# A hybrid diffusion layer on one core: HGRN2's backward direction held in reversed order, scores by 64-row products, split tiles moved to 64 bytes modulo 128

## The chip, the cores and the metric

The kernel runs on one core of one Trainium2 chip. The metric is the device time of one execution in microseconds (us), lower is better.

## The reference, cut to what matters

One layer serves 256 context tokens and 2048 latent tokens of width 1024. `h = RMSNorm(x) * (1 + scale) + shift`, `z = h @ w_in` feeds four groups of heads (convolution, gMLP, HGRN2, S5), their outputs go through `w_out`, and a squared-ReLU MLP of width 4096 follows. Almost all arithmetic is in the matrix products. The part that the change rewrites is HGRN2, a linear recurrence with a forget gate, run forwards and backwards over the same `q` and `v`:

```python
def step(S, inp):
    qc, kc, vc, lf = inp
    b = jnp.cumsum(lf, axis=1)
    b_end = b[:, -1]
    inter = jnp.einsum('blhk,bhkv->blhv', qc * jnp.exp(b), S)
    decay = jnp.where(lower, jnp.exp(diff), 0.0)
    scores = jnp.einsum('bthk,bshk,btshk->bhts', qc, kc, decay)
    intra = jnp.einsum('bhts,bshv->bthv', scores, vc)
    ...
o_f, s_f = hgrn_scan(q, k_f, v, lf_f, s0[:, 0])
o_b, s_b = hgrn_scan(jnp.flip(q, 1), jnp.flip(k_b, 1), jnp.flip(v, 1), jnp.flip(lf_b, 1), s0[:, 1])
```

## The kernel before, in words

**Split products.** Every large product is in three parts: each operand is split into `hi` (rounded to fp32r) and `lo` (the rest), and `gemm_cm` (L185) adds hi*hi, lo*hi and hi*lo for eight slices of 128, so one output of 128 x n takes 24 matmuls at lines L192 to L194. The weights' unit (`whl`, four buffers) is the stationary operand, the tokens' `hi` and `lo` tiles are the moving one, n = 512 columns for a latent block and 256 for the context block. In `gemm_tm` (L576, L579 to L581) and in pass 2's L1096 to L1098 it is the other way round: `whl` moves, and a 128-column slice of the tokens' tile is stationary.

**Blocks and stages.** There are five blocks: the context (256 tokens) and four latent ones (512 each). Pass 1 makes q, v and the gates of HGRN2 and the S5 input and runs `hgrn_local` (L735) for each block and each of two pairs of heads, ten times in all; this lies at about 190 to 630 us. Pass 2 and the S5 scan follow to about 1050 us. From then on it is `mix_out`, `mlp_up` and `mlp_down`: block 0 first (256 columns wide), then blocks 1 to 4. Per latent block `mix_out` has 8 outputs, and each of four quarters has 8 of `mlp_up` and 8 of `mlp_down`; the last quarter of the last block is done in two halves of 256 columns.

**HGRN2 inside a chunk.** `hgrn_local` holds both directions at once, forward in partitions 0 to 63 and backward in 64 to 127, on tiles of 128 x 1024 (two heads by 512 tokens; 512 wide for the context). Scores in a chunk of 128 are built in seven levels (cs = 1, 2, ... 64). In each level a copy `z` of q is made in which the half that must not count is zero (`qz` and `qzr`; ScalarE at L780 and L781, zeros by GpSimd at L778 and L779); eight matmuls of 128 rows, 128 x 128 out, follow (L787); kt is multiplied by the decays in two halves (VectorE for the forward rows, GpSimd for the backward rows, both L791), q likewise (VectorE, L792 and L793), and the scores of the level are taken out of PSUM under a mask (L808, all 1024 columns) or, in the last two levels, by copies (L806). Two instances are interleaved by hand with the products of the next pairs (L1375 on), and the tile framework orders each engine's queue from a simulated timeline.

```python
            A.activation(v4(z, 0, 64, 1), v4(q, 0, 64, 1), AF.Copy)
            A.activation(v4(z, 64, 128, 0), v4(q, 64, 128, 0), AF.Copy)
            ...
                    PE.matmul(sc[:, s_], kt[:, s_], z[:, s_], start=True, stop=True)
```

**Queues.** SyncE issues nearly all DMAs. `hgrn_local` loads q from qn by four DMAs of 64 partitions (L749) and stores q by one (L810).

**Where tiles lie.** Pools are stacked from the low end of a partition (left) or from its high end (right), each tile rounded up to 32 bytes. By that count `whl` starts at 64 modulo 128. The `hi` and `lo` tiles of `hp` (pass 1, pass 2, and block 0's `mix_out`), `h30` (block 0's MLP) and `h3b` (`mlp_down`'s input, blocks 1 to 4), all on the right, start at 96 modulo 128. Those of `h3a`, on the left, which hold the input of `mix_out` and `mlp_up` for blocks 1 to 4, start at 0 modulo 128.

Of the kernel before, what the change touches and what calls it, by code (L numbers as in the profile page):

```python
# [36 lines left out]
CH = 128  # L37
# [37 lines left out]
def trunk_kernel(ctx, tc, I, O):  # L75
# [28 lines left out]
    def psc():  # L104
        return psums["s"].tile([128, 1024], F32, tag="ps", name=nm("psc"))
# [498 lines left out]
    def f_out(b, h, ps, f):  # L604
        n = BLOCKS[b][1]
        v = f[:, (h % 2) * n:(h % 2 + 1) * n]
        A.activation(v, ps[:, :n], AF.Sigmoid)
        A.activation(v, v, AF.Identity, bias=lb[:, h:h + 1], scale=omlb[:, h:h + 1])
# [13 lines left out]
    def pass1_g(b, pair, hs, p1):  # L622


        n = BLOCKS[b][1]
        ps = pg()
        gemm_cm(ps, n, kept_unit("w_p1c", 3 * pair), hs)
        qn = q_out(b, ps, p1)
        f = f_tile(p1)
        for hh in range(2):  # L630
            ps = pg()
            gemm_cm(ps, n, kept_unit("w_p1c", 3 * pair + 1 + hh), hs)
            f_out(b, 2 * pair + hh, ps, f)
        return qn, f
# [100 lines left out]
    def hgrn_local(b, pair, qn, f, vt, p1, qz, Sx, masks_):  # L735
# [6 lines left out]
        def w(tag):  # L742
            return p1.tile([128, 1024], F32, tag=tag, name=nm(tag), bufs=2)

        kt, q, at = w("kt"), w("q"), w("at")
        f = f[:, :n2]
        for hh in range(2):
            for d in range(2):
                SP.dma_start(q[64 * d:64 * d + 64, hh * n:(hh + 1) * n], qn[hh * 64:hh * 64 + 64, :n])  # L749
        G.tensor_scalar(kt[:, :n2], f, -1.0, 1.0, ALU.mult, ALU.add)  # L750
        V.tensor_scalar(f, f, F_MIN, None, ALU.max)
        sc = psc()
        for i in range(m2):
            s_ = slice(i * 128, i * 128 + 128)
            PE.matmul(sc[:, s_], kt[:, s_], q[:, s_], start=True, stop=True)
# [6 lines left out]
        for lv in range(7):  # L762
# [3 lines left out]
            def v4(t, lo_, hi_, half):  # L766
                return t[lo_:hi_, :n2].rearrange("p (m two c) -> p m two c", two=2, c=cs)[:, :, half, :]
# [3 lines left out]
            def tb(lo_, hi_, half):  # L771
                return tv[lo_:hi_, :, half:half + 1].to_broadcast([64, mm, cs])

            if lv < len(qz):
                z = qz[lv]
            else:
                z = p1.tile([128, 1024], F32, tag="qzr", name=nm("qzr"), bufs=2)
                G.memset(v4(z, 0, 64, 0), 0.0)  # L778
                G.memset(v4(z, 64, 128, 1), 0.0)  # L779
            A.activation(v4(z, 0, 64, 1), v4(q, 0, 64, 1), AF.Copy)  # L780
            A.activation(v4(z, 64, 128, 0), v4(q, 64, 128, 0), AF.Copy)  # L781
            sc = psc()
# [32 lines left out]
        A.activation(kt[:, :n2], pt[:, :n2], AF.Copy)  # L815
# [242 lines left out]
    def pass2(b, p2, hp, hs, Sx, gates, gmg, gmw, gmb):  # L1058
# [29 lines left out]
        sr = p2.tile([128, 8], F32, tag="sr", name=nm("sr"))  # L1088
# [226 lines left out]
    psum(ctx, g=3, a=1)  # L1315
    e2 = ExitStack()
# [3 lines left out]
    with ExitStack() as e1:  # L1320
# [292 lines left out]
```

## Time and profile before

| what | value |
|---|---|
| median of 3 runs | 2869.5 us (2867.88 to 2870.06) |
| profiled execution's own time | 2869.65 us |
| span of the trace (first to last instruction) | 2867.9 us, so 1.75 us lie around it |
| mean granted TensorE clock | 0.98 |
| busy shares | TensorE 95%, weight load 78%, VectorE 66%, ScalarE 39%, GpSimd 32% |

PE is TensorE's matmul, PEld its weight load, DVE VectorE, ACT ScalarE, POOL GpSimd, SP SyncE. Matmuls overlap and their ends are modelled, so the time of a matmul in a stream is read from start to start, not from its duration. An fp32 matmul shows as two records, an fp32r one as one.

### The profile page before, as it was taken

To read this page: it belongs to the slowest core of one execution; us is meant where nothing else is said; L and a number is where in the kernel's file an instruction comes from. 1 tells how busy PE (TensorE), PEld (TensorE's weight loads), DVE (VectorE), ACT (ScalarE), POOL (GpSimd) and SP (SyncE) were. 2 spreads that over 40 slices of the span, in tenths; PEclk is the share of its full clock that TensorE was granted. 3 is DMA by queue.
4 is the path that set the end of the run, shared out by engine and by line. 5 is a ranking of instruction groups with operands and counts; after the bars stand their busy time and mean duration, and the time that the engine had idled before them with its cause. 6 is when DMAs were issued, how large, how long until landed. Compare 5 with 4: busy or idle time off the path is not lost.

```text
span 2867.9 us, 38038 instructions
## 1 busy us (share of the span) xinstructions
PE 2711.8 (95%) x14376; PEld 2247.5 (78%) x14376; DVE 1887.3 (66%) x2766; ACT 1109.4 (39%) x1710; POOL 915.7 (32%) x807
## 2 busy tenths in 40 slices
PE   6798999899999869999999999999999999999998
PEld 3576878887777759987788888788887888888888
DVE  8879677966799986669873474943474334553336
ACT  4645454541432535442422343333343223433223
POOL 4435234622443533343221242211432111411113
PEclk8899999999999989999999999999999999999999
DMA  7884555678887746633333443333343334333334
GB/s 263 281 293 151 173 192 175 224 275 320 288 291 246 240 165 212 185 114 113 113 103 96 125 143 107 111 96 107 113 148 101 99 95 126 95 125 96 96 96 126
DMA packets 186279, 467.17 MB, mean 163 GB/s; under 512 B 40176, under 2 KB 70000, under 8 KB 173040
## 3 DMA queue, kind: packets, MB, share of 16 engines
q1 hardware_dynamic: 183936, 463.56, 49.3%
q8 instruction: 114, 1.87, 0.3%
q10 hardware_dynamic: 2160, 1.18, 0.1%
q14 instruction: 69, 0.57, 0.1%
HBM read 383.47 MB, written 77.53 MB: 161 GB/s over the span
## 4 chain that ended last, share of the span: by engine, by line
PE 59%; DVE 12%; DMA 3%; issue 1%; ACT 0%; POOL 0%; SPq 0%; DVEq 0%; ACTq 0%
PE pg L194 19%; PE pg L193 19%; PE pg L192 19%; DVE x L1184 3%; DVE m L997 1%; DVE whl L162 1%; DVE gg L1005 1%; DVE hh L1014 1%; DVE pa L289 1%; DMA x<-uD 1%; DMA whl<-w_p2c_hl 1%; DVE hh L1013 0%; DMA x<-in_xT_dram 0%; DVE lo L304 0%; PE pb L1051 0%
## 5 line engine op out<-in xcount | busy, mean ns | idle before, releaser
L194 PE MATMUL pg<-hi,whl 128*128 128x512 f32 (+1 forms) x3488 | 1287.5, 370 | 8.3 <-DVE whl L162 8.2
L192 PE MATMUL pg<-hi,whl 128*128 128x512 f32 (+1 forms) x3488 | 1284.8, 371 | 10.0 <-ACT whl L156 3.5
L193 PE MATMUL pg<-lo,whl 128*128 128x512 f32 (+1 forms) x3488 | 1287.2, 370 | 4.6 <-DVE lo L1245 3.0
L160 POOL TENSOR_TENSOR whl<-wraw,whl 128x512 fp32r<-128x512 f32 (+1 forms) x296 | 434.2, 1488 | 1199.7 <-ACT whl L156 1133.4
L192 PEld LDWEIGHTS pg<-hi,whl 128*128 128x128 f32 x3488 | 658.2, 189 | 133.0 <-issue 6.6
L193 PEld LDWEIGHTS pg<-lo,whl 128*128 128x128 f32 x3488 | 659.2, 189 | 129.3 <-issue 7.4
L194 PEld LDWEIGHTS pg<-hi,whl 128*128 128x128 f32 x3488 | 659.3, 189 | 127.3 <-DVE whl L162 8.9
L156 ACT ACTIVATE whl<-wraw 128x1024 fp32r<-128x1024 f32 (+1 forms) x396 | 415.5, 1052 | 600.6 <-PE pg L194 459.0
L162 DVE TENSOR_TENSOR whl<-wraw,whl 128x1024 fp32r<-128x1024 f32 x248 | 309.5, 1249 | 65.2 <-ACT whl L156 63.7
L1257 DVE SCALAR_TENSOR_TENSOR x<-pg,adaT,x 128x512 f32<-128x512 f32 (+1 forms) x168 | 111.7, 668 | 290.6 <-PE pg L194 290.3
L1242 DVE TENSOR_TENSOR t<-t 128x512 f32<-128x512 f32 (+1 forms) x160 | 115.7, 724 | 252.4 <-ACT t L1241 252.0
L1241 ACT ACTIVATE t<-pg 128x512 f32<-128x512 f32 (+1 forms) x160 | 88.6, 554 | 367.8 <-PE pg L194 365.4
L1184 DVE SCALAR_TENSOR_TENSOR x<-x,cvw 128x512 f32<-128x512 f32 (+1 forms) x300 | 216.2, 764 | 0.6
L1245 DVE TENSOR_TENSOR lo<-t,hi 128x512 fp32r<-128x512 f32 (+1 forms) x160 | 142.6, 892 | 36.2 <-ACT hi L1244 36.1
L791 POOL TENSOR_TENSOR kt<-kt,tnx 64x256 f32<-64x256 f32 (+1 forms) x120 | 98.7, 830 | 173.8 <-issue 132.7
L252 POOL TENSOR_TENSOR sq<-sq,sq 128x512 f32<-128x512 f32 (+1 forms) x56 | 87.6, 1563 | 124.0 <-ACT sq L248 124.0
L1244 ACT ACTIVATE hi<-t 128x512 fp32r<-128x512 f32 (+1 forms) x160 | 93.0, 582 | 82.8 <-DVE t L1242 82.8
L1225 DVE SCALAR_TENSOR_TENSOR x<-pg,adaT,x 128x512 f32<-128x512 f32 (+1 forms) x40 | 27.8, 694 | 108.6 <-PE pg L194 108.5
L248 ACT ACTIVATE sq<-x 128x512 f32<-128x512 f32 (+1 forms) x120 | 66.0, 553 | 77.3 <-DVE sq L252 17.3
L787 PE MATMUL psc<-qzr,kt 128*128 128x128 f32 x576 | 76.8, 286 | 10.5 <-DVE kt L791 7.2
L787 PEld LDWEIGHTS psc<-qzr,kt 128*128 128x128 f32 x576 | 72.6, 201 | 14.5 <-POOL kt L791 7.9
L303 ACT ACTIVATE hi<-hm,adaT 128x512 fp32r<-128x512 f32 (+1 forms) x72 | 49.5, 697 | 67.3 <-DVE hm L301 63.3
(371 smaller groups left out, 2913.2 us busy)
## 6 DMA issues: line engine op xcount, KB each, us to landing
wraw<-in_mlp_w_dram SPq DMA_DIRECT2D x328, 512.0 KB, 3.6
whl<-w_p2c_hl SPq DMA_DIRECT2D x32, 1024.0 KB, 7.5
whl<-w_p1c_hl SPq DMA_DIRECT2D x22, 1024.0 KB, 7.6
wraw<-in_w_out_dram SPq DMA_DIRECT2D x40, 512.0 KB, 3.6
awt<-in_ada_w_dram SPq DMA_DIRECT2D x32, 512.0 KB, 6.1
whl<-w_p1t_hl SPq DMA_DIRECT2D x12, 1024.0 KB, 5.0
x<-in_xT_dram SPq DMA_DIRECT2D x16, 512.0 KB, 5.8
aw<-in_ada_w_dram SPq DMA_DIRECT2D x8, 1024.0 KB, 6.6
```

The source lines that it names most:

```text
L156: A.activation(hi[:, :w], raw[:, :w], AF.Copy)
L160: G.tensor_tensor(lo[:, h_], raw[:, h_], f32(hi[:, h_]), ALU.subtract)
L162: V.tensor_tensor(lo[:, :w], raw[:, :w], f32(hi[:, :w]), ALU.subtract)
L192: PE.matmul(ps[:, :n], wh, xh[:, ts], start=k == 0, stop=False)
L193: PE.matmul(ps[:, :n], wh, xl[:, ts], start=False, stop=False)
L194: PE.matmul(ps[:, :n], wl, xh[:, ts], start=False, stop=k == 7)
L787: PE.matmul(sc[:, s_], kt[:, s_], z[:, s_], start=True, stop=True)
L791: eng.tensor_tensor(kv, kv, tb(lo_, hi_, 1 - half)[:, hs_, :], ALU.mult)
L1184: V.scalar_tensor_tensor(acc[i][:, :n], u2[:, i, k:k + n], cvw[:, i, k:k + 1], acc[i][:, :n], ALU.mult, ALU.add)
L1242: V.tensor_tensor(r, r, r, ALU.mult)
L1245: V.tensor_tensor(lo, r, f32(hi), ALU.subtract)
L1257: V.scalar_tensor_tensor(x8[:, o, ts], ps[:, :n], adaT[:, 40 + o, c:c + 1], x8[:, o, ts], ALU.mult, ALU.add)
```

## The change

The backward half of every tile of `hgrn_local` is held in reversed order inside each chunk of 128, so that both directions use the same halves at a level. q is loaded twice: qx (both directions in plain order, for the first product) and q (backward half reversed, from qr). kx holds kt's backward half in plain order, remade at each level. Each level's eight products of 128 rows become sixteen of 64 rows, 64 columns each, the forward ones from partitions 0 to 63 and the backward ones from 64 to 127, into different PSUM banks. The zeroed copies of q are gone. The update of kt is one VectorE operation on 128 partitions in place of one on VectorE and one on GpSimd, that of q one in place of two. The transposes at the end are in halves of 64 rows. Apart from that three small tiles move others: `edge` (32 bytes) at the high end moves all right-hand pools by 32 bytes, so `hp`, `h30` and `h3b` start at 64 modulo 128; `pad` (64 bytes) moves `h3a` from 0 to 64; `sr` grows from 32 to 64 bytes, which leaves the tiles of `p2` below it at multiples of 64.

```diff
     def q_out(b, ps, p1):
...
-        return qn
+        qr = p1.tile([128, 512], F32, tag="qr", name=nm("qr"))
+        A.activation(turn(qr, 0, 128, 0, n), chunks(qn, 0, 128, 0, n), AF.Copy)
+        return qn, qr
...
-        A.activation(v, ps[:, :n], AF.Sigmoid)
+        A.activation(v[0:64], ps[0:64, :n], AF.Sigmoid)
+        A.activation(chunks(f, 64, 128, a, a + n), turn(ps, 64, 128, 0, n), AF.Sigmoid)
...
         for hh in range(2):
             for d in range(2):
-                SP.dma_start(q[64 * d:64 * d + 64, hh * n:(hh + 1) * n], qn[hh * 64:hh * 64 + 64, :n])
+                for q_, src in ((qx, qn[0]), (q, qn[d])):
+                    SP.dma_start(q_[64 * d:64 * d + 64, hh * n:(hh + 1) * n], src[hh * 64:hh * 64 + 64, :n])
...
+        A.activation(kx[0:64, :n2], kt[0:64, :n2], AF.Copy)
+        A.activation(chunks(kx, 64, 128, 0, n2), turn(kt, 64, 128, 0, n2), AF.Copy)
...
-                z = p1.tile([128, 1024], F32, tag="qzr", name=nm("qzr"), bufs=2)
-                G.memset(v4(z, 0, 64, 0), 0.0)
-                G.memset(v4(z, 64, 128, 1), 0.0)
-            A.activation(v4(z, 0, 64, 1), v4(q, 0, 64, 1), AF.Copy)
-            A.activation(v4(z, 64, 128, 0), v4(q, 64, 128, 0), AF.Copy)
...
+            def score(d, i):
+                o_ = sc[:, 512 * d + 64 * i:512 * d + 64 * i + 64].rearrange("p (r c) -> p r c", c=cs)
+                s_ = slice(i * 128, i * 128 + 128)
+                if d:
+                    PE.matmul(o_, kt[0:64, s_], v4(q[0:64, s_], 1), start=True, stop=True)
+                else:
+                    PE.matmul(o_, kx[64:128, s_], v4(q[64:128, s_][:, ::-1], 0), start=True, stop=True)
...
                 for i in range(hh * m, hh * m + m):
-                    s_ = slice(i * 128, i * 128 + 128)
-                    PE.matmul(sc[:, s_], kt[:, s_], z[:, s_], start=True, stop=True)
+                    for d in (1, 0):
+                        score(d, i)
...
-                for eng, lo_, hi_, half in ((V, 0, 64, 0), (G, 64, 128, 1)):
-                    kv = v4(kt, lo_, hi_, half)[:, hs_, :]
-                    eng.tensor_tensor(kv, kv, tb(lo_, hi_, 1 - half)[:, hs_, :], ALU.mult)
-            V.tensor_tensor(v4(q, 0, 64, 1), v4(q, 0, 64, 1), tb(0, 64, 0), ALU.mult)
-            V.tensor_tensor(v4(q, 64, 128, 0), v4(q, 64, 128, 0), tb(64, 128, 1), ALU.mult)
+                kv = v4(kt[:, :n2], 0)[:, hs_, :]
+                V.tensor_tensor(kv, kv, tb(1)[:, hs_, :], ALU.mult)
+            A.activation(v5(kx, 1), v5(kt, 0)[:, :, ::-1, ::-1], AF.Copy)
+            V.tensor_tensor(v4(q[:, :n2], 1), v4(q[:, :n2], 1), tb(0), ALU.mult)
...
-                V.copy_predicated(a3, masks_[:, lv, :].unsqueeze(1).to_broadcast([128, m2, 128]), s3)
+                    V.copy_predicated(a5, m5.to_broadcast([128, m2, 64 // cs, cs]),
+                                      s3.rearrange("p m (r c) -> p m r c", c=cs))
...
-        SP.dma_start(qD[b][:, 2 * pair:2 * pair + 2, :], q[:, :n2].rearrange("p (h t) -> p h t", h=2))
+        qo = p1.tile([128, 1024], F32, tag="qo", name=nm("qo"))
+        A.activation(chunks(qo, 64, 128, 0, n2), turn(q, 64, 128, 0, n2), AF.Copy)
+        for lo_, q_ in ((0, q), (64, qo)):
+            SP.dma_start(qD[b][lo_:lo_ + 64, 2 * pair:2 * pair + 2, :],
+                         q_[lo_:lo_ + 64, :n2].rearrange("p (h t) -> p h t", h=2))
...
-            PE.transpose(pt[:, i * 128:i * 128 + 128], kt[:, i * 128:i * 128 + 128], ident)
+            PE.transpose(pt[:, i * 64:i * 64 + 64], kt[0:64, s_], ident[0:64, 0:64])
+            PE.transpose(pt[:, 512 + i * 64:512 + i * 64 + 64], kx[64:128, s_], ident[64:128, 64:128])
...
-        sr = p2.tile([128, 8], F32, tag="sr", name=nm("sr"))
+        sr = p2.tile([128, 16], F32, tag="sr", name=nm("sr"))
...
+    edge = pool(ctx, "edge", side="right").tile([128, 8], F32, tag="edge", name="edge")
+    G.memset(edge, 0.0)
...
+    pad = pool(e5, "pad").tile([128, 16], F32, tag="pad", name="pad")
+    G.memset(pad, 0.0)
     h3a = pool(e5, "h3a", 9)
```

The masked copy at levels 0 to 4 is now done twice (d = 1, 0), each on half of the columns; the copies of levels 5 and 6 keep their number.

## Rows read from the trace of the kernel before

**Rows 1.** The page: busy time by engine, and the granted clock in 40 slices.
```profile
PE 2711.8 (95%) x14376; PEld 2247.5 (78%) x14376; DVE 1887.3 (66%) x2766; ACT 1109.4 (39%) x1710; POOL 915.7 (32%) x807
...
PEclk8899999999999989999999999999999999999999
```
**Rows 2.** Busy time by stage: window, PE, PEld, DVE, ACT, POOL; clock, DMA share, GB/s.
```profile
190.00:640.00 450.00, 405.69 (x2654) 357.75 (x2655) 360.87 (x645) 221.50 (x386) 183.32 (x238) 0.96 0.58 200
640.00:1050.00 410.00, 373.50 (x2475) 300.57 (x2474) 348.96 (x577) 143.71 (x284) 157.95 (x168) 0.97 0.77 260
...
1210.00:2790.00 1580.00, 1574.89 (x6883) 1275.28 (x6882) 863.41 (x963) 531.35 (x703) 406.09 (x267) 1.00 0.35 110
```
**Rows 3.** Line L193 in a stretch of mlp_up, mlp_down, block 0: count, min/median/max, first to last start.
```profile
L193 PE MATMUL pg<-lo,whl x64: 392/392/392, 1960.8 to 2004.1; 128*128 128x512 f32 x64
...
L193 PE MATMUL pg<-lo,whl x64: 389/394/397, 1916.0 to 1960.1; 128*128 128x512 f32 x64
...
L193 PE MATMUL pg<-lo,whl x315: 277/278/281, 1090.0 to 1199.9; 128*128 128x256 f32 x158
```
**Rows 4.** Timeline, TensorE: first and last of 22, then of 41 matmuls with whl moving.
```profile
361.55 0.40 PE L579 MATMUL pg<-whl,hi 128*128 128x512 f32 x1
...
366.45 0.39 PE L581 MATMUL pg<-whl,hi 128*128 128x512 f32 x1
...
814.38 0.28 PE L1096 MATMUL pg<-whl,hi 128*128 128x256 f32 x1
...
819.12 0.28 PE L1097 MATMUL pg<-whl,lo 128*128 128x256 f32 x1
```
**Rows 5.** Groups by line, 190 to 640 us: busy, mean ns, idle before, releasers.
```profile
L791 POOL TENSOR_TENSOR kt<-kt,tnx 64x256 f32<-64x256 f32 (+1 forms) x120 | 98.7, 830 | 173.8 <-issue 132.7 <-PE psc L787 32.9 <-DVE Sl L856 5.9
L787 PE MATMUL psc<-qzr,kt 128*128 128x128 f32 x576 | 76.8, 286 | 10.5 <-DVE kt L791 7.2 <-ACT kt L815 2.1 <-DVE at L808 0.8
...
L808 DVE COPY_PREDICATED at<-masks,psc 128x1024 f32<-128x1024 int32 (+1 forms) x50 | 60.5, 1210 | 0.0
L791 DVE TENSOR_TENSOR kt<-kt,tnx 64x256 f32<-64x256 f32 (+1 forms) x120 | 57.2, 491 | 27.3 <-PE psc L787 26.4
...
L793 DVE TENSOR_TENSOR q<-q,tnx 64x512 f32<-64x512 f32 (+1 forms) x59 | 45.1, 766 | 1.7
...
L780 ACT ACTIVATE qzr<-q 64x512 f32<-64x512 f32 (+1 forms) x40 | 23.5, 587 | 45.4 <-DVE q L792 23.8 <-PE psc L787 18.8 <-POOL kt L791 2.6
```
**Rows 6.** TensorE's waits, 190 to 640 us: us in total, times, longest.
```profile
PE psc L787 <- DVE kt L791: 10.1, 6, 2.9
PE psc L787 <- DVE at L808: 8.5, 8, 3.8
```
**Rows 7.** Timeline, TensorE: into and out of the 64-column products, and 64 columns moving.
```profile
353.95 0.40 PE L192 MATMUL pg<-hi,whl 128*128 128x512 f32 x1
354.28 0.85 PEld L820 LDWEIGHTS psc<-at,vt 128*64 128x64 f32 x16 [0.37 <-issue]
354.28 1.09 PE L820 MATMUL psc<-at,vt 128*64 128x128 f32 x16
355.30 0.52 PEld L787 LDWEIGHTS psc<-qzr,kt 128*128 128x128 f32 x4 [0.17 <-issue]
...
359.30 1.89 PE L829 MATMUL psc<-vt,kt 128*128 128x64 f32 x16
```
**Rows 8.** Groups by line and shape: masked copies; a reversed (L991) and a plain copy.
```profile
L808 DVE COPY_PREDICATED at<-masks,psc 128x1024 f32<-128x1024 int32 x40 | 53.3, 1332 | 0.0
...
L991 ACT ACTIVATE d<-pd 64x512 f32<-64x512 f32 x16 | 9.5, 593 | 0.2
L990 ACT ACTIVATE d<-pd 64x512 f32<-64x512 f32 x16 | 9.4, 589 | 20.7 <-PE pd L986 20.7
...
L808 DVE COPY_PREDICATED at<-masks,psc 128x512 f32<-128x512 int32 x10 | 7.2, 724 | 0.0
```
**Rows 9.** DMA issues, 190 to 640 us: KB each, median us to landing.
```profile
q<-qn SPq DMA_DIRECT2D x24, 128.0 KB, 2.5
```

More of the change, by code (lines that the diff above doesn't have):

```diff
@@ L592, in vt_tile, with chunks, turn @@
         return p1.tile([128, 4, 256], F32, tag="vt", name=nm("vt"), bufs=2)
+    def chunks(t, lo_, hi_, a, e):
+        return t[lo_:hi_, a:e].rearrange("p (m t) -> p m t", t=CH)
+    def turn(t, lo_, hi_, a, e):
+        return chunks(t, lo_, hi_, a, e)[:, :, ::-1]
     def q_out(b, ps, p1):
@@ L605, in f_out @@
         n = BLOCKS[b][1]
[L606 to L607 removed]
+        a = (h % 2) * n
+        v = f[:, a:a + n]
+        A.activation(v[0:64], ps[0:64, :n], AF.Sigmoid)
+        A.activation(chunks(f, 64, 128, a, a + n), turn(ps, 64, 128, 0, n), AF.Sigmoid)
         A.activation(v, v, AF.Identity, bias=lb[:, h:h + 1], scale=omlb[:, h:h + 1])
@@ L733, in trunk_kernel, with hgrn_local @@
     first = []
-    def hgrn_local(b, pair, qn, f, vt, p1, qz, Sx, masks_):
+    def hgrn_local(b, pair, qn, f, vt, p1, Sx, masks_):
         t0, n, c = BLOCKS[b]
@@ L743, in w @@
             return p1.tile([128, 1024], F32, tag=tag, name=nm(tag), bufs=2)
-        kt, q, at = w("kt"), w("q"), w("at")
+        kt, q, at, kx = w("kt"), w("q"), w("at"), w("kx")
+        qx = p1.tile([128, 1024], F32, tag="qx", name=nm("qx"))
         f = f[:, :n2]
@@ L754, in hgrn_local @@
             s_ = slice(i * 128, i * 128 + 128)
-            PE.matmul(sc[:, s_], kt[:, s_], q[:, s_], start=True, stop=True)
+            PE.matmul(sc[:, s_], kx[:, s_], qx[:, s_], start=True, stop=True)
         V.tensor_tensor(q[:, :n2], q[:, :n2], f, ALU.mult)
@@ L764, in hgrn_local, with v4, v5 @@
             mm = n2 // (2 * cs)
-            def v4(t, lo_, hi_, half):
-                return t[lo_:hi_, :n2].rearrange("p (m two c) -> p m two c", two=2, c=cs)[:, :, half, :]
+            def v4(t, half):
+                return t.rearrange("p (m two c) -> p m two c", two=2, c=cs)[:, :, half, :]
+            def v5(t, half):
+                return t[64:128, :n2].rearrange("p (m r two c) -> p m r two c", m=m2, two=2, c=cs)[:, :, :, half, :]
             tv = tcur.rearrange("p (m two) -> p m two", two=2)
-            def tb(lo_, hi_, half):
-                return tv[lo_:hi_, :, half:half + 1].to_broadcast([64, mm, cs])
@@ L774, in hgrn_local, with tb @@
-            if lv < len(qz):
-                z = qz[lv]
-            else:
-                z = p1.tile([128, 1024], F32, tag="qzr", name=nm("qzr"), bufs=2)
-                G.memset(v4(z, 0, 64, 0), 0.0)
-                G.memset(v4(z, 64, 128, 1), 0.0)
-            A.activation(v4(z, 0, 64, 1), v4(q, 0, 64, 1), AF.Copy)
-            A.activation(v4(z, 64, 128, 0), v4(q, 64, 128, 0), AF.Copy)
+            def tb(half):
+                return tv[:, :, half:half + 1].to_broadcast([128, mm, cs])
@@ L1370, in trunk_kernel @@
         masks_ = const("masks", [128, 5, 128], I["masks"], I32, p1, SP)
-        qz = [p1.tile([128, 1024], F32, tag=f"qz{lv}", name=f"qz{lv}") for lv in range(3)]
-        for z in qz:
-            G.memset(z, 0.0)
         prev = None
         for i in range(2 * NB):
-            cur = hgrn_local(P1_ORDER[i // 2], i % 2, *ready[i], p1, qz, Sx, masks_)
+            cur = hgrn_local(P1_ORDER[i // 2], i % 2, *ready[i], p1, Sx, masks_)
             for _ in range(5):
```

20 lines of the change are left out of this document (13 added, 7 removed).

## The prediction, made before the changed kernel had run

> **What bounds the kernel now.** The page's busy shares and clock slices come first: TensorE is busy for 95% of the span and, after the first fifth or so, its clock stands at the full 2.4 GHz level [rows 1]. The table by stage says where that is a bound. From 1210 to 2790 us TensorE is busy 1574.89 of 1580 us while VectorE has 863.41 [rows 2]: that is more than half of the span, and there any time off a matmul comes off the end. In pass 1 (190 to 640 us) TensorE is busy 405.69 of 450 us, so 44 us are idle, and VectorE 360.87; in pass 2 and the scan (640 to 1050 us) VectorE has 348.96 and TensorE 373.50 of 410, and neither alone is the bound [rows 2].
>
> The third view is what a matmul costs in a stream. L193 is every third matmul. In a stretch of mlp_up its 64 starts run from 1960.8 to 2004.1 us: 43.3 us over 63 x 3 steps, 229.1 ns each. In mlp_down they run from 1916.0 to 1960.1: 44.1 over 189, 233.3 ns [rows 3]. Engine, shape, clock, weights' tile and code are the same; the moving tile lies at 0 modulo 128 in the first and at 96 in the second. In block 0, moving tile at 96 and 256 columns, 315 starts take 109.9 us: 116.7 ns, half of 233.3 [rows 3], so the loss goes with the columns that stream. 512 columns at 2.4 GHz would be 213.3 ns.
>
> **The tile offsets.** This is the large part. The change makes the pair (moving, weights) 64/64 in every split product; before it is 0/64 (229.1), 96/64 (233.3) and, where whl moves, 64/96. That last pair takes 4.90 us over 21 steps, 233.3 ns, at 512 columns, and 4.74 over 40, 118.5 ns, at 256 [rows 4]. So 64/64 is in no row. Its bounds are 213.3 ns (columns at full clock) and 233.3 (the slowest pair seen). All three pairs fit one reading: what counts is how far the two tiles are out of step. 32 bytes out costs 233.3 whichever operand is off, 64 bytes out 229.1; in step would be one more step of 4.2, some 224.9. I take 226, most of that step, as it lies nearest to the 0/64 row. For 256 columns I take half, 113.
>
> Counts by the code: mlp_up and mix_out of blocks 1 to 4, 4 x (768 + 192) = 3840 matmuls at 0; mlp_down of the same, 4 x 768 less 192 = 2880 of 512 columns at 96; block 0 (1728) and the split last quarter (384) make 2112 of 256 columns at 96. Gains: 2880 x 7.3 ns = 21.0 us; 3840 x 3.1 = 11.9; 2112 x 3.7 = 7.8. Pass 1 has about 840 products of 512 columns (504 at L192 to L194, 336 at L579 to L581): 840 x 7.3 = 6.1, times the 0.9 of the time that TensorE is busy there, 5.5. Pass 2 has 768; with VectorE as busy as it is, I count a fifth of 5.6, so 1. In the tail nothing else comes up: VectorE's 55% and a DMA share of 0.35 leave room [rows 2]. Sum 47. Each ns by which 64/64 is off my 226 moves the end by 8.7 us (6720 matmuls, half of 2112, nine tenths of 840, a fifth of 768).
>
> **HGRN2, TensorE.** 504 score matmuls of 128 rows become 1008 of 64 rows. Two records each, as before. With 64 columns moving and 128 columns of weights, 16 records took 1.89 us, about 0.11 each [rows 7]; L787's undisturbed step, with 128 moving, is the same 0.11 (its 0.29 is the modelled duration) [rows 5]. If forward and backward halves run side by side, the total stays 504 x 2 x 0.11 = 111 us; if they follow each other it is 222. Halves of columns do run side by side: 16 records of L820, each 128 columns twice over (107 ns at 2.4 GHz), took 1.09 us instead of 1.7 [rows 7]. No row shows halves of rows; I take side by side, and the doubling is a rival. The price of going in and out of half-array products is in the same rows: from the last 128-row matmul to the first of L820 0.33 us instead of 0.23, and 0.17 us of idle weight load after it [rows 7], so 0.27 for a group. The timeline has L787 in 57 groups between other products: 57 x 0.27 = 15 us more. The transposes' 64-row halves I cost at nothing (72 become 144 with half the columns; bounds a few us either way).
>
> **HGRN2, the other engines.** VectorE loses one of the two q updates per level: 70 operations of about 0.76 us, 52 us less [rows 5]. The masked copy becomes two of half width: 2 x 0.724 against 1.332 us [rows 8], 40 times, 5 more; the ten narrower ones add 1. kt's update costs VectorE the same count and loses its GpSimd partner (98.7 us in 120 operations, 0.83 each) [rows 5]. ScalarE loses 140 copies of z (0.59 each [rows 5], some 82 us) and gets 70 reversed copies to kx; a reversed copy costs what a plain one does, 593 against 589 ns [rows 8], so 40 us, and with kx's first copies, qo, qr and the second sigmoid about 83 in all: no change, on an engine with 221.50 of 450 us [rows 2]. SyncE gets 40 more q loads and 10 more q stores; a load takes 2.5 us [rows 9], one more group is queued ahead of the next weights' loads, and at a DMA share of 0.58 [rows 2] it lies under products. If that cover went, it would be 2.5 us for each of ten tiles.
>
> What this is worth is TensorE's idle time in pass 1, 44 us. The waits behind it are named: kt on VectorE 10.1 us, the masked copy 8.5 [rows 6], and L780 waited 23.8 us for the q update [rows 5], which now feeds the product with no copy between. The new link is kt to kx to the backward product, 0.6 us of ScalarE per level, with ScalarE's queue behind it. Bounds: 0 to 40 us back; I take 15, near the named waits' sum. It pays for the 15 of the switches. HGRN2 comes out at 0, from -30 to +20.
>
> **Sum.** 2869.65 (the profiled execution: its span of 2867.9 and 1.75 around it; it stands 0.15 above the median of 2869.5) - 47 + 0 = 2822 us.
>
> **Rivals.**
> *64/64 is as good as 0/64, no better* (only the 32 byte step matters): 229.1 everywhere, 3.1 x 8.7 = 27 later, 2849. For: 64/96 at 256 columns costs 118.5, more than half of its 233.3, as if the weights' 32 bytes added a fixed amount there and the moving 64 were as good as 0 [rows 4].
> *64 is as slow as 96*: 7.3 x 8.7 = 63 later, 2886, slower than before, since h3a's 3840 lose 4.2 each. For: the only rows with a moving tile at 64 stand at 233.3 [rows 4]. Against: their weights lie at 96. It decides from 231.4 ns up.
> *The offset does nothing*; h3a is fast for another reason: 2870. The Trainium skill, SBUF — State Buffer (Specifications), gives 16-byte lines, with a penalty for each access that crosses to a new one; 0, 64 and 96 are all whole lines, and by that the tiles' places would change nothing. Rows 3 speak against it: 229.1 and 233.3 with only the tile differing.
> *64-row halves follow each other*: 111 us more on TensorE in pass 1, of which its idle time takes up some 20: about 90 later, 2912. Against: L820. For: loads of two halves share one path in no row that I have. The Trainium skill, TensorE: Matmul & The Clock Gate (LDWEIGHTS), says that a load's time goes with its columns and not its rows, so a 64-row load would be no shorter; L829's 0.11 for 64 columns moving agrees that the load is what counts there.
>
> **How the numbers follow.** Chances: my case 0.50, as good as 0/64 0.24, nothing 0.08, as slow as 96 0.11, halves in turn 0.07. Over 0.2% (5.7 us, about what a measurement of this kernel tells from no change) faster: 0.49 + 0.23 + 0.02 = 0.74; slower 0.11 + 0.07 + 0.01 = 0.19; within 0.07. My case's own range is 2800 to 2845 (223.5 to 228.6 ns). The whole: down to 2788, where 64/64 is 222, and up to 2886, where it is 233.3; left out are the halves in turn and a still faster pair.
>
> **What would show it.** L193 from start to start in mlp_up and mlp_down: one value for both, 226; 229.1, 233.3 or two different values name the rival. The window of the MLP, 1580 us now, would be shorter by some 34. In pass 1, forward and backward records starting within some 10 ns of each other; L787's successor in groups of 16 records per half level in 0.9 us, not 1.8; GpSimd's share falling by 100 us and more; VectorE's by about 45. The prediction is wrong if the MLP keeps its length, or if pass 1 grows by over 20 us.

## The result, and the profile after

The changed kernel takes 2943.51 us (median of 4 runs, 2938.39 to 2943.9) against 2869.78 for the kernel before beside it: 1.0257 times as long, 95% interval 1.0244 to 1.0269. The forecast was 2822. The profiled execution took 2943.9 us, its span is 2941.8. Two things went otherwise than forecast: TensorE's clock fell in HGRN2, and the new tile offsets were worth nothing.

The page of the changed kernel answers to [rows 1]:

```profile
PE 2786.3 (95%) x15456; PEld 2318.1 (79%) x15456; DVE 1808.9 (61%) x2746; ACT 1109.9 (38%) x1698; POOL 747.8 (25%) x586
...
PEclk8897889879999989999999999999999999999999
```

VectorE lost 78 us and GpSimd 168, more than forecast, but the clock's eights and sevens now reach into the ninth slice and TensorE's busy time rose by 74. The table by stage (columns as in [rows 2], with block 0's start as one row more) says where:

```profile
190.00:640.00 450.00, 413.86 (x3322) 363.85 (x3321) 269.20 (x539) 199.70 (x322) 24.70 (x20) 0.83 0.52 167
640.00:1050.00 410.00, 382.07 (x2508) 306.78 (x2508) 301.06 (x554) 134.54 (x277) 129.79 (x144) 0.96 0.81 281
1050.00:1210.00 160.00, 134.44 (x997) 125.33 (x996) 135.15 (x191) 73.63 (x121) 67.25 (x54) 0.89 0.56 187
1210.00:2790.00 1580.00, 1576.34 (x7188) 1294.26 (x7187) 886.36 (x995) 549.85 (x738) 415.63 (x275) 1.00 0.36 114
```

From 190 to 640 us the granted clock was 0.83 in place of 0.96. The trace's clock records know two levels, 0.5 and 1.0 (1.2 and 2.4 GHz), so a mean of 0.83 is (1 - 0.83) x 2 x 450 = 153 us at 1.2 GHz, before some 34. Over the whole trace these records add up to 295.6 us at 1.2 GHz, before 119.5. Half of the 176 more, 88 us, is TensorE work lost, beside a loss of 74 at the end. The last product of L581, which ends the products that are interleaved with HGRN2, ended at 545.5 us in place of 480.9.

Line L193 from start to start, in mlp_down, mlp_up and block 0, answers to [rows 3]; one row from each of three windows:

```profile
L193 PE MATMUL pg<-lo,whl x46: 389/389/389, 1595.0 to 1625.6; 128*128 128x512 f32 x46
...
L193 PE MATMUL pg<-lo,whl x54: 392/395/398, 1635.3 to 1672.4; 128*128 128x512 f32 x54
...
L193 PE MATMUL pg<-lo,whl x342: 283/283/283, 1160.1 to 1282.8; 128*128 128x256 f32 x171
```

mlp_down: 30.6 us over 135 steps, 226.7 ns. mlp_up: 37.1 over 159, 233.3. Block 0: 122.7 over 1023, 119.9. All three have moving tile and weights at 64 modulo 128, and I had forecast one value for each width, 226 and 113. Modulo 256 they differ: the weights lie at 192, h3b, hp and h30 at 192 too, h3a at 64.

The next view is the clock around one level of HGRN2, by windows (columns as above):

```profile
212.00:226.00 14.00, 14.00 (x116) 11.93 (x115) 5.53 (x12) 2.53 (x4) 0.00 (x0) 1.00 0.34 105
227.00:231.00 4.00, 3.57 (x64) 3.42 (x62) 4.00 (x8) 0.78 (x2) 0.00 (x0) 1.00 0.86 241
233.00:248.00 15.00, 14.64 (x137) 14.16 (x137) 10.76 (x19) 7.92 (x14) 0.00 (x0) 0.50 0.22 56
```

From 212 to 226.5 us TensorE ran 512-column products with two groups of score products and one of first products (L771) between them, at full clock. From 226.78 to 246.4 it ran 64-row score products and nothing else, and in that run, at 231.9 us, the clock went to 0.50. Just ahead of the fall TensorE had waited for VectorE, which the middle row, ending at 231, hardly shows:

```profile
230.30 0.27 PE L803 MATMUL psc<-q,kx 64*128 64x64 f32 x1
231.88 0.38 PE L801 MATMUL psc<-q,kt 64*128 64x64 f32 x1 [1.32 <-DVE tnx L820]
```

So the fall itself may need the wait. What the wait does not explain is that the clock stayed down: from 233 to 248 us, score products until 246.4, PE counts as busy for 14.64 of 15 us, at 0.50. Nine of the twelve falls between 190 and 640 us lie inside such a run, in which no products of full size come between; none of the twelve ended before products of full size had come again, and they last 12.8 us in the mean, where the eight falls of the kernel before last 4.3. TensorE's timeline shows the end of a group of score products at full clock, and later in pass 1 what the low clock does to other products:

```profile
255.22 0.27 PE L801 MATMUL psc<-q,kt 64*128 64x64 f32 x1
255.23 0.27 PE L803 MATMUL psc<-q,kx 64*128 64x64 f32 x1
255.33 0.27 PE L801 MATMUL psc<-q,kt 64*128 64x64 f32 x1
255.34 0.27 PE L803 MATMUL psc<-q,kx 64*128 64x64 f32 x1
255.44 0.27 PE L801 MATMUL psc<-q,kt 64*128 64x64 f32 x1
255.45 0.27 PE L803 MATMUL psc<-q,kx 64*128 64x64 f32 x1
255.65 0.50 PE L579 MATMUL pg<-whl,hi 128*128 128x512 f32 x1
...
419.79 0.63 PE L579 MATMUL pg<-whl,hi 128*128 128x512 f32 x1
420.22 0.63 PE L580 MATMUL pg<-whl,lo 128*128 128x512 f32 x1
420.65 0.63 PE L581 MATMUL pg<-whl,hi 128*128 128x512 f32 x1
```

A product of pass 1 takes 0.43 us from start to start where [rows 4] had 0.23. The score products themselves are as forecast: a forward and a backward record start 10 ns apart, a pair every 0.11 us, and 16 products (32 records) take 1.73 us from first to last start at full clock, near the 1.67 of eight 128-row ones.

### The profile page after: what moved, and what is told of

It reads as the page before. It is cut to its first block, busy times and chain, and to the rows that moved or that the text cites. A ratio compares the mean times of both kernels' runs of the same rounds, so it can differ in the third digit from the quotient of the medians.

```text
span 2941.8 us, 39878 instructions
## 1 busy us (share of the span) xinstructions
PE 2786.3 (95%) x15456; PEld 2318.1 (79%) x15456; DVE 1808.9 (61%) x2746; ACT 1109.9 (38%) x1698; POOL 747.8 (25%) x586
## 4 chain that ended last, share of the span: by engine, by line
PE 75%; DVE 12%; DMA 4%; ACT 2%; issue 2%; SPq 1%; POOL 0%; DVEq 0%; ACTq 0%
PE pg L193 21%; PE pg L192 21%; PE pg L194 21%; PE psc L801 2%; DVE x L1216 2%; DVE at L832 1%; PE pg L579 1%; PE pg L581 1%; DVE m L1029 1%; PE pg L580 1%; DVE whl L162 1%; PE psc L803 1%; PE psc L861 1%; DVE lo L304 1%; DVE pa L289 1%
## 5 line engine op out<-in xcount | busy, mean ns | idle before, releaser
L192 PE MATMUL pg<-hi,whl 128*128 128x512 f32 (+1 forms) x3488 | 1287.4, 372 | 25.1 <-ACT st L586 10.0
L193 PE MATMUL pg<-lo,whl 128*128 128x512 f32 (+1 forms) x3488 | 1289.3, 370 | 3.9 <-DVE lo L1277 2.6
L194 PE MATMUL pg<-hi,whl 128*128 128x512 f32 (+1 forms) x3488 | 1288.1, 370 | 0.6 <-DVE whl L162 0.6
L192 PEld LDWEIGHTS pg<-hi,whl 128*128 128x128 f32 x3488 | 662.8, 190 | 150.7 <-ACT st L586 10.9
L160 POOL TENSOR_TENSOR whl<-wraw,whl 128x512 fp32r<-128x512 f32 (+1 forms) x296 | 427.2, 1464 | 1324.1 <-ACT whl L156 1266.8
L193 PEld LDWEIGHTS pg<-lo,whl 128*128 128x128 f32 x3488 | 663.8, 190 | 123.7 <-issue 5.3
L194 PEld LDWEIGHTS pg<-hi,whl 128*128 128x128 f32 x3488 | 663.6, 190 | 117.9 <-issue 4.6
L801 PE MATMUL psc<-q,kt 64*128 64x64 f32 x1008 | 165.3, 326 | 28.9 <-DVE at L832 15.6
L801 PEld LDWEIGHTS psc<-q,kt 64*128 64x128 f32 x1008 | 154.6, 238 | 40.9 <-issue 29.3
L803 PE MATMUL psc<-q,kx 64*128 64x64 f32 x1008 | 165.7, 327 | 0.0
L803 PEld LDWEIGHTS psc<-q,kx 64*128 64x128 f32 x1008 | 154.6, 238 | 2.8 <-issue 2.0
L811 DVE TENSOR_TENSOR kt<-kt,tnx 128x256 f32<-128x256 f32 (+1 forms) x120 | 48.0, 414 | 100.2 <-PE psc L801 83.9
```

The lines of the kernel that those rows point to most:

```text
L160: G.tensor_tensor(lo[:, h_], raw[:, h_], f32(hi[:, h_]), ALU.subtract)
L192: PE.matmul(ps[:, :n], wh, xh[:, ts], start=k == 0, stop=False)
L193: PE.matmul(ps[:, :n], wh, xl[:, ts], start=False, stop=False)
L194: PE.matmul(ps[:, :n], wl, xh[:, ts], start=False, stop=k == 7)
L801: PE.matmul(o_, kt[0:64, s_], v4(q[0:64, s_], 1), start=True, stop=True)
L803: PE.matmul(o_, kx[64:128, s_], v4(q[64:128, s_][:, ::-1], 0), start=True, stop=True)
```

## Experiments on the tile offsets

Each run's ratio is to the kernel before on the same chip. First the change was taken apart in two: the three tiles alone,

```diff
+    edge = pool(ctx, "edge", side="right").tile([128, 8], F32, tag="edge", name="edge")
...
-        sr = p2.tile([128, 8], F32, tag="sr", name=nm("sr"))
+        sr = p2.tile([128, 16], F32, tag="sr", name=nm("sr"))
...
+    pad = pool(e5, "pad").tile([128, 16], F32, tag="pad", name="pad")
```

> The kernel before with the three small tiles alone (edge, sr, pad); HGRN2 as before. Theory 'the moves cancel': what counts is the offset of the moving tile against the weights' modulo 256, not 128. The right-hand tiles then lie at 192, as the weights do, and h3a at 64. mlp_down of blocks 1 to 4 comes down from 233.3 to 226.7 ns (2880 matmuls, -19.2 us), mix_out and mlp_up of blocks 1 to 4 go up from 228.9 to 233.3 (3840, +16.9), the 256-column products go up from 116.8 to 119.9 (2112, +6.5), pass 1 gains some 5: in all -1, from 2864 to 2875 us, granted clock and half-rate time as in the kernel before (120 us at the 1.2 GHz level). Rival 'the moves gain what was predicted and HGRN2 loses it all': 2823 (-47). Rival 'the moves lose': the whole +74, 2943.

Measured: 2869.09 us, 0.9998 (0.9989 to 1.0007). The moves cancel: what one tile gains another loses.

The rest of the change, without the tiles (the three lines taken out of the changed kernel):

> The changed kernel without the three small tiles: the HGRN2 part alone. Theory 'the loss is in HGRN2 and is TensorE's clock': 2937 to 2949 us; in the window 190 to 640 us the granted clock stands near 0.83 and some 150 us are at the 1.2 GHz level, as in the changed kernel; the MLP's steps are the ones of the kernel before (228.9, 233.3, 116.8 ns). Rival 'HGRN2 is neutral, as predicted': 2870, with the clock at 0.96. Rival 'HGRN2 gains and the tiles lose': under 2860.

Measured: 2944.71 us, 1.0261 (1.0247 to 1.0275). The whole loss is in the HGRN2 part. Its row for 190 to 640 us has the changed kernel's clock:

```profile
190.00:640.00 450.00, 417.38 (x3333) 364.98 (x3332) 270.81 (x538) 201.40 (x323) 23.52 (x20) 0.83 0.52 167
```

Then the offsets by themselves. Kernel before, with h3a and h3b at the weights' own offset modulo 256:

```diff
+    pad = pool(e5, "pad").tile([128, 48], F32, tag="pad", name="pad")
...
     h3a = pool(e5, "h3a", 9)
...
+    edge = pool(e5, "edge", side="right").tile([128, 8], F32, tag="edge", name="edge")
...
     h3b = pool(e5, "h3b", 11, side="right")
```

> The kernel before, with h3b moved by 32 bytes (from 224 to 192 modulo 256) and h3a by 192 bytes (from 0 to 192), both then at the weights' own 192 modulo 256; the 256-column tiles (hp, h30) stay. Theory 'the same offset as the weights modulo 256 is the fast one': mlp_down 226.7 ns (-19.2 us), mix_out and mlp_up of blocks 1 to 4 226.7 in place of 228.9 (-8.4), the last quarter's 384 products of 256 columns +1.2: 2843 us, from 2840 to 2847. Rival 'modulo 128 counts and h3a was slow for another reason (its side, its buffers)': h3a at 192 is 64 modulo 128 and costs 233.3 as in the changed kernel, +16.9: 2869. Rival 'each tile at random': anything between.

Measured: 2845.75 us, 0.9918 (0.9904 to 0.9931). h3a, in a stretch of mlp_up (42.9 us over 189 steps, 227.0 ns):

```profile
L193 PE MATMUL pg<-lo,whl x64: 389/389/389, 1548.6 to 1591.5; 128*128 128x512 f32 x64
```

Other offsets, by the same three tiles (sizes in elements of 4 bytes): `edge` of 24 at the start (hp and h30 at 128), `pad` of 32 (h3a at 128) and an `edge` of 16 ahead of h3b (64):

> The kernel before with other tile offsets modulo 256 (weights at 192): hp and h30 (256 columns, and pass 1) from 224 to 128, h3b from 224 to 64, h3a from 0 to 128. Theory 'equal modulo 256 is best, half-way round is like 0, and the side does not matter': h3b at 64 takes 233.3 ns as h3a did there, whichever side it lies on; h3a at 128 (64 away from the weights, as 0 is) takes 228.9; so the blocks 1 to 4 stay as in the kernel before. For 256 columns at 128 no forecast closer than between 114.5 and 120: from -5 to +7 us. Together 2860 to 2878. Rival 'the right-hand side was the fast one': h3b at 64 takes 226.7, -19 us, 2850.

Measured: 2879.34 us, 1.0040 (1.0026 to 1.0053), 1.3 above the upper end. h3b, h3a and block 0:

```profile
L193 PE MATMUL pg<-lo,whl x31: 392/398/398, 1438.9 to 1459.9; 128*128 128x512 f32 x31
...
L193 PE MATMUL pg<-lo,whl x47: 394/394/394, 1556.3 to 1588.5; 128*128 128x512 f32 x47
...
L193 PE MATMUL pg<-lo,whl x295: 276/276/280, 1099.8 to 1199.8; 128*128 128x256 f32 x148
```

h3b at 64 takes 233.3 ns on the right side as h3a did on the left, so the side is out. h3a at 128 takes 233.3, not 228.9: "64 bytes away" is no rule. With 256 columns 128 is the best place so far, 113.4 ns. The sum agrees: 3840 x 4.2 ns = 16 more, 1728 x 3.3 = 6 less, about 10; measured 11.

The best of each, hp and h30 at 128, h3a and h3b at 192:

> The kernel before with tile offsets modulo 256 chosen by width (weights at 192): h3a and h3b (512 columns) at 192, hp and h30 (256 columns in block 0, pass 1) at 128. Theory 'each width has its own best offset, and the gains add': the 22.7 us that h3a and h3b at 192 gave, and block 0's 1728 products of 256 columns at 114.3 in place of 116.8 ns, 4.3 us, and some 1 from the products with whl moving: 28 below the kernel before, 2838 to 2843. Rival 'block 0 is bound by something else, or pass 1 loses': 2845 to 2848, as with h3a and h3b alone.

Measured: 2840.38 us, 0.9907 (0.9893 to 0.9922). The gains add. This version beats both kernels; it has nothing of the HGRN2 part.

Last, whether 192 is fast because it equals the weights' place:

```diff
+    shift = cst.tile([128, 16], F32, tag="shift", name="shift")
...
     hind = cst.tile([128, 2], F32, tag="hind", name="hind")
```

with h3a kept at 0 and h3b at 192.

> The kernel before with the weights' tiles moved by 64 bytes, from 192 to 0 modulo 256, h3a kept at 0 (so equal to the weights now) and h3b moved from 224 to 192 (64 below the weights); hp and h30 stay at 224. Theory 'equal to the weights is what is fast': h3a's mix_out and mlp_up take 226.7 ns in place of 228.9 (-8.4 us), and h3b, 64 below the weights as h3a was in the run with 128 against 192, 233.3 as before; the 256-column products stand 32 below the weights, which no run has shown, bounds 114.3 and 120 ns (-5 to +7 us): 2855 to 2868. Rival 'it is the place itself, 192, whatever the weights': h3b 226.7 (-19.2 us), h3a 228.9: 2844 to 2857. Rival 'both tiles count each by itself': neither value is 226.7.

Measured: 2863.84 us, 0.9981 (0.9972 to 0.9990). h3a and h3b (L195 is L193 there):

```profile
L195 PE MATMUL pg<-lo,whl x62: 389/389/389, 1466.0 to 1507.5; 128*128 128x512 f32 x62
...
L195 PE MATMUL pg<-lo,whl x47: 394/394/394, 1520.7 to 1552.9; 128*128 128x512 f32 x47
```

226.8 ns at 0 with the weights at 0, 233.3 at 192: equal offsets are the fast ones, not the place 192. All pairs seen, ns from start to start (256 columns of h3b from the split last quarter):

| moving less weights, modulo 256 | 512 columns | 256 columns |
|---|---|---|
| 0 | 226.7 (192/192 and 0/0) | 119.9 (192/192) |
| 64 | 228.9 (0/192) | not seen |
| 32 | 233.3 (224/192) | 116.7 (224/192) |
| 128 | 232.1 to 233.3 (64/192) | 118.7 (64/192) |
| 192 | 233.3 (128/192 and 192/0) | 113.4 (128/192), 116.0 in the mean (192/0) |
| 224 | 233.3 (224/0) | 118.3 (224/0) |

For 512 columns the difference settles it as far as it was tried: 0 and 192 were seen at two places each, the other differences at one. For 256 columns the mean of 116.0 is made of two rates; in the split last quarter of the last run, about 117.7 ns, then after a short break 113.3:

```profile
L195 PE MATMUL pg<-lo,whl x77: 281/281/281, 2806.0 to 2832.8; 128*128 128x256 f32 x77
...
L195 PE MATMUL pg<-lo,whl x51: 276/276/279, 2833.6 to 2850.6; 128*128 128x256 f32 x51
```

The pair 128/192 has the same two, 113.4 for most of block 0 and 117.8 for its last 144 products, so the two pairs do not contradict each other. What chooses between the rates is open.

## Experiments on the clock and HGRN2

The 64-row products alone, in the kernel before:

```diff
-            A.activation(v4(z, 0, 64, 1), v4(q, 0, 64, 1), AF.Copy)
-            A.activation(v4(z, 64, 128, 0), v4(q, 64, 128, 0), AF.Copy)
...
-                    PE.matmul(sc[:, s_], kt[:, s_], z[:, s_], start=True, stop=True)
+                    for d in (1, 0):
...
+                        PE.matmul(o_, kt[p_, s_], qv, start=True, stop=True)
```

> The kernel before with only the 128-row score products of each level replaced by two of 64 rows and 64 columns (kt and q read in plain order, no zeroed copies, masked copy in two halves); no reversed order, no kx, qx, tiles where they were, kt's and q's updates on VectorE and GpSimd as before. Theory 'the 64-row products bring the 1.2 GHz level': over 80 us more at that level in pass 1 than the 34 of the kernel before, and the end comes 30 to 75 us later, 2900 to 2945 us. Rival 'the clock falls because of the new order of work (one engine's update ahead of both directions, more waits)': the clock in 190 to 640 us stays near 0.96 and the time is 2850 to 2875.

Measured: 2981.10 us, 1.0389 (1.0375 to 1.0403), a larger loss than I gave, with 324.3 us at 1.2 GHz in all. Its row:

```profile
190.00:640.00 450.00, 387.55 (x2989) 339.35 (x2987) 311.27 (x519) 111.91 (x194) 116.50 (x127) 0.81 0.41 143
```

Reversed order, kx and the added DMAs are not in it, so none of them is needed for the loss of clock.

The other way round, all of the change but these products:

```diff
...
-                    for d in (1, 0):
-                        score(d, i)
+                    o_ = 512 * hh + 128 * (i - hh * m)
+                    PE.matmul(sc[:, o_:o_ + 128], (kt, kx)[i % 2][:, i * 128:i * 128 + 128],
+                              q[:, i * 128:i * 128 + 128], start=True, stop=True)
```

> The changed kernel, but each level has eight score products of 128 rows and 128 columns again (kt and kx in turn stationary, q moving), as many and as large as in the kernel before; all else of the change stays. It leaves out the right scores: what it computes there is no score. Theory 'the loss is TensorE's clock, and 64-row, 64-column products bring it': the 1.2 GHz level falls from 296 us to 120-150 us in all, the granted clock in 190 to 640 us is near 0.96, and the time comes down by 70 to 90 us, to 2850-2870. What it then stands below the kernel before with the same tiles (2869) is what the lighter VectorE and GpSimd are worth. Rival 'reversed order, kx's copy, the doubled masked copies and the added DMAs hold pass 1 up': the time stays above 2920 with the clock at 0.96. Rival 'the clock follows something else in the changed order': it stays near 0.83 and the time near 2940.

Measured: 2857.49 us, 0.9965 (0.9953 to 0.9976), 155.0 us at 1.2 GHz.

```profile
190.00:640.00 450.00, 413.24 (x2836) 367.15 (x2836) 303.08 (x638) 227.33 (x389) 28.59 (x25) 0.97 0.65 216
```

The clock is back (0.973 to 0.976 over the whole of each of the eight executions, 0.950 to 0.955 for the changed kernel; the traced one, of 2866.37 us, was the longest). The medians put all the rest of the HGRN2 rewrite 11.6 us below the run with the tiles alone (2869.09), with scores that are not right.

Rows or columns? First 128 rows with 64 columns (`PE.matmul(o_, (kt, kx)[i % 2][:, s_], v4(q[:, s_], 1), ...)`, eight per level):

> The changed kernel, but each level has eight products of 128 rows and 64 columns (full rows, half the columns; no right scores: half of the score products is left out). Tells rows from columns. Theory 'few columns per product': the clock falls as in the changed kernel, over 230 us at 1.2 GHz, 2900 to 2945 us. Rival 'half the rows': the clock stays as in the kernel before, under 160 us at 1.2 GHz, and the time is 2845 to 2870.

Measured: 2877.52 us, 1.0030 (1.0014 to 1.0046), 210.1 us at 1.2 GHz, between the two forecasts.

```profile
190.00:640.00 450.00, 420.08 (x2729) 373.82 (x2729) 295.81 (x620) 220.42 (x369) 27.31 (x22) 0.91 0.63 210
```

Then 64 rows with 128 columns (`PE.matmul(sc[:, o_:o_ + 128], (kx, kt)[d][p_, s_], q[p_, s_], ...)`, sixteen per level):

> The changed kernel, but its sixteen 64-row products per level stream all 128 columns (outputs that overlap; no right scores). The other way round: half the rows, full columns. Theory 'few columns per product': the clock comes back, under 170 us at 1.2 GHz, and the time to 2860-2890. Rival 'half the rows': over 230 us at 1.2 GHz and 2920 to 2970 us. If both this and the run with 128 rows and 64 columns stay slow, either one is enough.

Measured: 2914.05 us, 1.0163 (1.0142 to 1.0184), 182.4 us at 1.2 GHz.

```profile
190.00:640.00 450.00, 412.94 (x3649) 354.49 (x3647) 295.49 (x618) 219.03 (x365) 25.90 (x22) 0.95 0.59 197
```

Half the columns alone bring 55 us more at 1.2 GHz than the full products, half the rows alone 27, both together, in the changed kernel, 141. (The six traces here that leave HGRN2 as it was read from 119.5 to 143.1, so some 25 us say little.) The time of this run fits neither forecast: the clock is nearly whole, yet it is 57 us above the full products. TensorE's queue differs between the two: 953 products of L192 to L194 stand ahead of the last score product with full products, 864 here, 843 in the changed kernel. So the order of the queue, which the tile framework's planner sets, had to be told apart from the clock, by one line in each of the two kernels:

```diff
-        step(second, 2)
+        with tc.high_priority():
+            step(second, 2)
```

> The changed kernel, with one thing else: the first two steps of pass 2 have a higher priority in the planner, so that 926 of the products at L192 to L194 stand ahead of the last score product in TensorE's queue in place of 843 (936 in the kernel before). Theory 'part of the loss is the order: products of pass 2 that lay between HGRN2's levels now come after it': 83 products of 0.23 us, 19 us: 2918 to 2930. Rival 'those products only change places with HGRN2, and the clock is all': HGRN2 ends later by as much as the rest is shorter, 2938 to 2948.

Measured: 2947.68 us, 1.0274 (1.0260 to 1.0288). The rival holds: at the low clock the order is worth nothing. HGRN2's last transpose starts at 693.8 us in place of 676.3, and what follows is 10.5 shorter.

> The run with 64 rows and 128 columns (clock near full in pass 1, 2914; no right scores), with the same higher priority for the first two steps of pass 2: 947 of the products at L192 to L194 ahead of the last score product in place of 864, nearly as in the run with full products (953, 2857). Theory 'with the clock up, order and switches make the rest': 19 us less, 2890 to 2900, and what then stays against the run with full products, 33 to 43 us, is 63 groups of 64-row products by 0.26 us for going in and out (16), the 19 us more that its groups last because they wait inside, and the little that the clock still loses. Rival 'the order costs nothing': 2910 to 2918.

Measured: 2883.39 us, 1.0051 (1.0037 to 1.0065), 31 us less where I gave 19; 42 us fewer at 1.2 GHz (140.4) came with it. The rows of these two, the changed kernel with that line and the 64 x 128 kernel with it:

```profile
190.00:640.00 450.00, 411.06 (x3348) 361.17 (x3347) 266.11 (x523) 205.84 (x332) 27.64 (x22) 0.84 0.53 175
```

and

```profile
190.00:640.00 450.00, 417.67 (x3701) 359.72 (x3699) 292.90 (x620) 221.61 (x368) 26.09 (x22) 0.97 0.63 207
```

They have the same priority and differ only in the columns that a score product streams, 64 against 128 (a full-clock group of sixteen takes 1.73 us in the one and 1.78 in the other). The one that streams fewer takes 64.3 us longer, with a clock of 0.84 against 0.97: (0.97 - 0.84) x 450 = 58 us of TensorE's work in this window alone. And 140.4 us at 1.2 GHz are no more than the 155.0 of the full products: half the rows alone, in this order, cost no clock.

One rival is left, that TensorE's waits in pass 1 bring the low level whatever it runs. By the two rows it stands idle for 39 us with 64 columns and for 32 with 128; the kernel before, with 44 idle, had 0.96 [rows 2]. The clock of the 64 x 128 kernel falls after waits too, but comes back. Here TensorE had waited 3.91 us, then ran score products alone:

```profile
252.08 0.55 PE L801 MATMUL psc<-q,kt 64*128 64x128 f32 x1 [3.91 <-DVE at L830]
```

and, in windows,

```profile
252.00:255.00 3.00, 2.92 (x27) 2.95 (x29) 3.00 (x6) 0.49 (x1) 0.74 (x1) 0.50 0.02 5
255.20:258.00 2.80, 2.33 (x29) 1.86 (x27) 2.44 (x6) 2.29 (x3) 0.00 (x0) 1.00 0.33 72
```

The clock was full again at 255.1 us, while score products still ran. With 64 columns it stayed at 0.50 through the whole run from 233 us on. So the waits go with the falls in both, and the small products keep the clock down. The loss comes apart, medians in us:

| kernel | median | step |
|---|---|---|
| tile moves alone | 2869.1 | |
| and the change with 128 x 128 products | 2857.5 | -11.6, the rest of the rewrite (scores not right) |
| products of 64 rows and 128 columns, with the priority | 2883.4 | +25.9, half-array products |
| products of 64 rows and 64 columns, with the priority | 2947.7 | +64.3, the clock |
| the changed kernel | 2943.5 | -4.2, the order: not clear of noise |

The ratios of the last two, 1.0274 and 1.0257, have intervals that overlap. The 25.9: by the starts in these traces, going into a group of 64-row products costs 0.318 us in place of 0.227 and coming out 0.202 in place of 0.031, so 0.26 a group; 64 groups are 17 us. The groups themselves last 14 us longer in all (134.2 against 120.1): some 7 because sixteen products take 1.78 us where eight take 1.67, and the rest in waits, above all for VectorE's masked copies, with 64 rows

```profile
PE psc L801 <- DVE at L830: 13.8, 12, 3.9
```

and with 128

```profile
PE psc L800 <- DVE at L825: 8.0, 7, 2.2
```

Together that is 31 us, so not all of it reaches the end.

Last, whether the 11.6 us can be had with right scores: 128-row products on zeroed copies again, in the reversed order, with the best offsets.

```diff
+            A.activation(v4(z[0:64, :n2], 1), v4(q[0:64, :n2], 1), AF.Copy)
+            A.activation(v5(z, 0), v5(q, 1)[:, :, ::-1, ::-1], AF.Copy)
...
+                    PE.matmul(sc[:, s_], kx[:, s_], z[:, s_], start=True, stop=True)
...
+            G.tensor_copy(v4(kx[0:64, :n2], 0), v4(kt[0:64, :n2], 0))
```

> The changed kernel's reversed order and its lighter VectorE work, but scores by eight products of 128 rows, so that no 64-row products are left in the levels: kx holds both directions in plain order (forward half copied by GpSimd), a zeroed copy z of q is made again by ScalarE (its backward half turned back), zeros by GpSimd, one masked copy; tile offsets as in the run with offsets chosen by width. Theory 'what the change saves on VectorE is worth the 11.6 us that the run with full products and no right scores stood below the one with the tile moves alone, and the copies lie on engines with room': about 11 us below the offsets alone, 2826 to 2834. Rival 'the longer chain of copies in each level (VectorE, then ScalarE and GpSimd, then TensorE) eats it': 2838 to 2850 with more waits of TensorE for kx and z.

Measured: 2876.91 us, 1.0023 (1.0014 to 1.0032): 36.5 above the offsets alone. Neither theory: the waits that the rival named are small. TensorE's waits from 476 to 720 us have one row for kx:

```profile
PE psc L805 <- POOL kx L809: 1.7, 1, 1.7
```

Up to the last product of L581 the two kernels are level (476.1 us against 478.9); HGRN2's end is 15 us later and what follows 17 longer. Part of it is again the clock, after HGRN2 this time. From 644 to 1050 us this kernel has

```profile
644.00:1050.00 406.00, 357.91 (x2247) 281.03 (x2243) 316.55 (x536) 123.99 (x245) 146.19 (x164) 0.92 0.74 250
```

and the one with the offsets alone

```profile
644.00:1050.00 406.00, 365.62 (x2425) 292.84 (x2424) 352.22 (x577) 142.78 (x278) 161.56 (x170) 0.97 0.77 264
```

Over the whole traces that is 194.2 against 132.1 us at 1.2 GHz, some 31 us of TensorE's work. Why the clock falls there, with no 64-row score products near, was not followed and stays open.

## Why the prediction was wrong, point by point

**What bounds the kernel** held: TensorE is the bound, and the loss is a loss of TensorE's time.

**The tile offsets, "64/64 in every split product, 226 ns" and "for 256 columns half, 113"**: this step failed. The three pairs of [rows 3, 4] do fit "how far out of step" modulo 128, but they fit modulo 256 as well, and I took the smaller period without a row that told them apart. For h3b the forecast value was right (226.7); for h3a, 128 bytes from the weights and so in step modulo 128 but not modulo 256, the rival "64 is as slow as 96" was (233.3); and 256 columns are not half of 512 (119.9). In place of -47 us the terms are 2880 x -6.6 ns = -19 us, 3840 x 4.2 = +16, 2112 x 3.2 = +7, and some -5 in pass 1: about nothing, as measured. [Rows 4] held a warning that I read as a rival only: 64/96 took 233.3 with 512 columns and 118.5 with 256, so the widths did not follow one rule. The Trainium skill's 16-byte lines (SBUF — State Buffer, Specifications) would have given no effect of the moves; the total agrees by accident, the streams (226.7 to 233.3 ns with only the place differing) do not.

**HGRN2 on TensorE, "the total stays" and "57 switches, 15 us"**: both held at full clock, 1.73 us a group and 0.26 us a switch. The Trainium skill, TensorEngine Tiling (Array Packing), Key Properties, says that tiles of the array load and multiply in parallel and that a change of tiling drains the engine. The trace agrees with the first (the pairs 10 ns apart); of the second it shows the price, 0.26 us, and not what makes it. The rival "halves follow each other" came nearest in time (2912) with a mechanism that the pairs 10 ns apart refute.

**The step that is missing** is the clock: "HGRN2 comes out at 0, from -30 to +20" has no term for it, and it is 64 of the 74 us. I read in [rows 1] that it was full after the first fifth, took this as a property of the stage, and never asked whether the new products would keep it. The reading was too kind already: a 9 in [rows 1] is 90% or more, and [rows 2] had 0.96 in pass 1, some 34 us at 1.2 GHz. The Trainium skill, TensorE: Matmul & The Clock Gate (Part 1), ties the level to how busy the engine has been. The trace agrees in part: TensorE had waited ahead of the fall at 231.9 us. But from 233 to 248 us PE counts as busy for 14.64 of 15 us and the level stays low, so busy time as the page of the profile counts it does not show the danger.

**HGRN2's other engines, "15 us won back"** was near in size: 11.6 with the clock up, in a kernel without right scores. That the lighter VectorE and GpSimd make these 11.6 is argued, not shown; with right scores on 128 rows they did not come. VectorE fell by 78 us and not 46, though a half masked copy costs more than the 0.724 that I took from [rows 8]: L832 has 0.95 us at 512 columns. Where the rest of its fall comes from was not followed. The added loads and stores of SyncE cost nothing that the run with full products shows.

**Sum.** -47 should have been 0, and HGRN2's 0 was +74: -12 for the rest of the rewrite, +26 for half-array products, +64 for the clock, and -4 that is not clear of noise.

## What to carry to other kernels

Before splitting a matmul into small ones, look at the granted clock of the stage and ask what the engine does when it has only the new ones to run: a form that costs the same per group can halve the rate of all that follows it. When a price depends on an address, vary one tile's place over the full period, for each width, before fitting a rule to three points; here equal offsets of moving tile and weights modulo 256 were worth 23 us at 512 columns for two spare tiles. And run the parts of a change apart: here one of them was worth nothing and the other all.

## What the runs showed of the hardware that was not expected

- Products of 64 rows that stream 64 columns, two at a time, keep TensorE at 1.2 GHz once it stands there, though PE counts as busy (14.64 of 15 us): 295.6 us of the execution against 155.0 with 128 x 128 products in the same places. Half the columns alone do less (210.1); half the rows alone 182.4, and 140.4 with the priority, which is no more than the full products.
- An fp32r stream of 512 columns takes 226.7 ns a product when moving tile and weights start at the same offset modulo 256 (two places seen), 228.9 with the moving tile 64 bytes on, 232 to 233.3 at the four other differences tried. 256 columns follow another order, 113.4 to 119.9 ns, whose best was a difference of 192, with 113.4 in some stretches and about 117.7 in others.
